# The order of a first mixer's end: sums, a pause of VectorE, two turned banks read late, and a weight block in another tile

## The chip, the cores and the metric

The kernel runs on one core of one Trainium2 chip, as one program. The metric is the device time of one execution in microseconds (us). Five engines work side by side, each through its own queue in order: TensorE (PE; matmuls and transposes, with its weight loads as PEld), VectorE (DVE), ScalarE (ACT), GpSimd (POOL) and SyncE (SP), which here only issues DMA transfers. An instruction starts when those ahead of it on its engine have started and the semaphores that it waits for are set.

## The reference

Two decoder layers on one sequence of 512 tokens and 1024 columns, in float32. Layer 0 mixes by pooling, layer 1 by a gated unit with a spatial matrix; each is followed by an MLP of 4096 hidden columns with squared ReLU.

```
for i in range(DEPTH):                      # DEPTH = 2
    mod = silu(c) @ ada_w[i] + ada_b[i]
    sh1, sc1, g1, sh2, sc2, g2 = jnp.split(mod, 6, axis=-1)
    h = modulate(rmsnorm(x, norm_mix_g[i]), sh1, sc1)
    y = pool_mixer(...) if i % 3 == 0 else sgu_mixer(...)
    x = x + g1[:, None, :] * y
    h = modulate(rmsnorm(x, norm_mlp_g[i]), sh2, sc2)
    x = x + g2[:, None, :] * square(relu(h @ mlp_w1[i])) @ mlp_w2[i]
return rmsnorm(x, final_g)
```

The change lies in layer 0: from the end of the pooling mixer, over the norm that follows it, into the first half of its MLP.

## The kernel before

**Products.** Every float32 product is made of three matmuls: each operand is split in a high part and the rest, and high × high, high × low and low × high are summed. ScalarE writes a weight block's high part (`wh`, L203), VectorE the rest (`wl`, by subtraction, L204). The tokens' operand is `hb`, `as` or `xh`, `xl`, made in the same two steps.

**The mixer.** A string of names, `WORK`, sets the order in which ScalarE, VectorE and TensorE get their instructions up to 60 us; `LOADS` gives the order of the transfers that SyncE issues. A name's letters say what is done, its digits which of four groups of 256 columns (or which column block) it is done for. `mGJ` and `nKJ` are products of 128 rows of the adaptive weights with the condition (VectorE, L420; the `n` are scale and shift of the MLP's column block K). `prG` is the pooling product (TensorE, L497), `adGH` adds it into the residual x for half H of the tokens (VectorE, L506), `smGT` squares the 256 columns G of token tile T and sums them (ScalarE, L333; with the suffix V on VectorE). `s` and `tot` sum over the groups (VectorE, L561 to L565), and `tot` starts the power -1/2 on GpSimd (L283), whose result is `rr`. `tnG` turns 256 columns of x in eight TensorE transposes into two banks `px` (L520), `tdG` reads them on ScalarE (L524). `diag` (L574, L576) spreads `rr` over diagonal matrices, which TensorE multiplies with ones into the bank `rb` (L577), so that the norm's factor stands beside each column. `nfK` makes mods and scale of block K on ScalarE (L540, L542). `hiK` and `loK` split the first MLP weights of block K (L551, L554). Ahead of `rb` and of the sweep TensorE runs some matmuls on constants (`busy`, L348).

**The sweep.** The MLP's row blocks 0 to 6 are computed together over eight steps, one for each column block k: 21 matmuls a step. Beside them VectorE and ScalarE make the operand of the next step: norm_hi (VectorE L581, then ScalarE L582), norm_lo (VectorE L586), norm_out (ScalarE L589), two `n`, the split of the next weights. After it `put` (L724) reads each bank with a ReLU into `g`, two halves a bank, in the order 3, 0, 1, 2, 4, 5, 6; then row block 7 follows (`f`), and squares (L716).

**The rest of the first half** goes in units (c, j, m) of a scheme with seven products in place of eight: block pair c, j, product m in the order 1, 5, 6, 3, 2, 7, 4. `b101q` is the bank of products for c = 1, j = 0. Their weights are sums of blocks: a chain tile `ch10q` or `ch11q` starts as block (0, 0), blocks are added into it by VectorE (L781), and one is added by a transfer of GpSimd's queue (L777), which can be issued only when `ch10q` has been read for the unit before. `raw1111q` is block (1, 1) of c = 1, j = 1 in row-block numbers r = 1, n = 1. Blocks lie in a pool of three tiles (`w4`), and some in the tile of the gate's row, which is free here (tag `gb`; the function `in_gb` says which). The `wh`, `wl` tiles are a pool of five. Within this part VectorE, ScalarE and the transfers' issues are put in order by the scheduler; TensorE's order is the program's.

Of the kernel before, what the change touches and what calls it, by code (L numbers as in the profile page):

```python
# [29 lines left out]
UNDER = 16  # L30

RESET = 48

POPS = (3, 3, 3, 2, 2, 1, 1, 1)

# [23 lines left out]
def c_g(n, k):  # L59
# [5 lines left out]

LOADS = """
    x m20 ag2 m22 m21 m23 gt11 pw2 gt10 m12 m10 m13 m11 m33 ag0 m01 pw1 m02 m00 m03 m32 m30 ag3 pw0 m31
    n11 pw3 raw0 n00 n21 n01 raw1
"""

WORK = """
    cab edge sq0 rowc sq2 sq3 sq1V rms m20 m22 rowp m21 m23 gt11 fin2 bandr gm2 win2 we2 gt10 pd2 win1 m12
    pr2 win3 m10 gc1 m11 bc1 ad21 m13 gm0 ad20 sm23 fin1 m33 we1 pd1 win0 m01 sm22 m02 m00 m03 pr1 ad10
    fin0 pd0 m32 gm3 m30 we0 pr0 m31 fin3 sm10 pd3 ad11 we3 sm21 sm11 hi0 pr3 sm20 ad00 sm13 sm12 sm01
    ad01 sm02 sm03 n00 tn2 sm00 tn0 ad30 s3 ad31 n01 sm30 sm31 sm33 sm32 td2 tot td0 tn3 nf0 n21 n11 tn1  # L80
    diag td3 td1 lo0
"""


GM = [0, 2, 3]
GT = [1]
# [5 lines left out]
def decoder_kernel(ctx: ExitStack, tc: tile.TileContext, xtok, vecs, rows, fgrow, ada0, adag, ada1, pool_w, w1s, w1f, w1b, w2, w_v, w_u, w_o, wsT, lnp, bs, out):  # L92
# [200 lines left out]
    with (  # L293
# [285 lines left out]
        def norm_hi(k):  # L579
            t = xf(k)  # L580
            V.scalar_tensor_tensor(t, t, scl[0][1][:, k : k + 1], rbs[0], ALU.mult, ALU.mult)  # L581
            A.activation(H(k, ALL)[0], t, AF.Identity, bias=mod(0, c_sh(1, k)))  # L582
# [15 lines left out]
            diag=spread_norms, hi=sweep_hi, lo=sweep_lo,  # L598
        )
        loads()  # L600
        for op in WORK.split():
            on_v, op = op.endswith("V"), op.rstrip("V")
            kind, d = op.rstrip("0123456789"), [int(c) for c in op if c.isdigit()]
            work[kind](*d, *([V] if on_v else []))
            loads()


        sweep = [bank("po", xz) for _ in range(SWEEP - 4)] + [bank("po") for _ in range(4)]
        busy("sweep", sweep[0])
        for k in range(KD):  # L610
            norm_hi(k)
            if k + 1 < KD:
                queue += [n for n in (f"n{k + 1}0", f"raw{k + 1}", f"n{k + 1}1") if n not in LOADS]
                loads()
                if f"n{k + 1}0" not in WORK:
                    n_(k + 1, 0)
                norm_lo(k)
                sweep_hi(k + 1)
                if f"n{k + 1}1" not in WORK:
# [12 lines left out]
            for f in range(EARLY):  # L632
                T.matmul(sweep[f], wl[:, fs[f]], xh, start=(k == 0), stop=False)
# [60 lines left out]
    def mlp(i, extra, units, final):  # L694
# [23 lines left out]
        def put(f, po):  # L718

            c, q = divmod(f, 8)  # L720
            j, p = divmod(q, 4)
            with tc.high_priority():
                for r in range(2):
                    A.activation(G_(c, r, j)[:, p], po[:, 256 * r : 256 * r + 256], AF.Relu)  # L724

        def squares(f):
            c, q = divmod(f, 8)
# [24 lines left out]
        spare = []  # L752

        def in_gb(c, j, r, n):
            return ((r, n) == (1, 0) and (i, c, j) != (1, 0, 0)) or (i, r, n, j) == (1, 1, 1, 1) and c < 2

        def blk(c, j, r, n):
            if (c, j, r, n) not in blks:
# [200 lines left out]
                more.setdefault(ss_[max(n - LEAD, 0)], []).append(at)  # L959
        real = [n for n, (k, u) in enumerate(units) if k in prep]  # L960
        ready = {}
        for n, (kind, u) in enumerate(units):
            if kind in calls:
                calls[kind](*u)
                continue
            if kind == "x":
                u()
                continue
            x = real.index(n)
            s = 0  # L970
# [392 lines left out]
```

## Time and profile before

| | |
|---|---|
| median of 3 runs | 843.9 us (842.48 to 845.34) |
| profiled execution | 844.26 us |
| its span | 842.6 us |
| granted TensorE clock, mean | 0.997 |
| busy: TensorE, its weight loads | 822.7 us, 727.4 us |
| busy: VectorE, ScalarE, GpSimd | 680.7, 514.9, 114.9 us |
| HBM read, written | 181.49 MB, 6.30 MB |

A row of a timeline gives start and duration in us, engine, line, operation, output<-inputs, shapes and how many like instructions are taken together; in brackets how long the engine stood idle ahead of it and what it then waited for. A row of the list of waits gives the waiting instruction, what it waited for, the time in total, how often, and the longest. Buffer numbers are left out of the names, so different blocks `ch10q` and tiles `g` read alike.

### The profile page before, as it was taken

What the parts mean: (1) busy time and instruction counts of PE and PEld (TensorE: products, weight loads), DVE (VectorE), ACT (ScalarE), POOL (GpSimd) and SP (SyncE); (2) the same over time, 40 slices, a digit from 0 to 9 for tenths busy, and PEclk for the clock granted to TensorE, in tenths of its full rate; (3) what the DMA queues carried; (4) which work ended last, traced back from release to release, by engine and by line L of the source; (5) the groups of instructions that cost most, each with busy time, mean ns of one, the idle gap of its engine ahead of it and who ended that gap; (6) DMA issues with size and microseconds to landing.
All of it is one profiled execution on the core that took longest, in us unless ns stands there. A gap on an engine that the chain in (4) does not pass through costs nothing.

```text
span 842.6 us, 12722 instructions
## 1 busy us (share of the span) xinstructions
PE 822.7 (98%) x4898; PEld 727.4 (86%) x4898; DVE 680.7 (81%) x864; ACT 514.9 (61%) x739; POOL 114.9 (14%) x135
## 2 busy tenths in 40 slices
PE   8999999999999999999999999999999999999996
PEld 7778899999988888888888887999999988888885
DVE  6889889988779867796898776688887678976886
ACT  5276786776755555676232237868677775665562
POOL 3010001000223300021020002011000132321000
PEclk9999999999999999999999999999999999999998
DMA  9999858998999989464856636568988799998502
GB/s 346 407 363 322 298 140 256 268 289 263 290 250 206 194 220 264 137 225 161 253 179 219 225 119 213 137 159 197 294 249 260 199 212 243 193 215 227 161 24 78
DMA packets 51651, 188.62 MB, mean 224 GB/s; under 512 B 5739, under 2 KB 5891, under 8 KB 50566
## 3 DMA queue, kind: packets, MB, share of 16 engines
q1 hardware_dynamic: 37090, 133.52, 43.9%
q0 software_dynamic: 14352, 54.02, 32.9%
q8 instruction: 38, 0.62, 0.3%
q10 hardware_dynamic: 148, 0.27, 0.1%
q14 instruction: 23, 0.19, 0.1%
HBM read 181.49 MB, written 6.30 MB: 223 GB/s over the span
## 4 chain that ended last, share of the span: by engine, by line
PE 65%; DVE 15%; DMA 10%; issue 4%; ACT 4%; POOL 1%; SPq 0%; POOLq 0%; DVEq 0%; ACTq 0%
PE pm L903 28%; PE po L216 12%; DVE wl L204 4%; DMA ada<-in_ada 3%; DMA wh<-in_ada 2%; PE b311q L216 2%; PE b305q L903 2%; PE b315q L903 2%; DVE ada L240 2%; PE b301q L216 2%; DVE ada L420 2%; PE b101q L216 1%; PE b315q L216 1%; PE b201q L216 1%; PE b305q L216 1%
## 5 line engine op out<-in xcount | busy, mean ns | idle before, releaser
L903 PE MATMUL pm<-wh,o 128*128 128x512 f32 x736 | 182.2, 390 | 0.0
L903 PEld LDWEIGHTS pm<-wh,o 128*128 128x128 f32 x736 | 137.8, 188 | 28.7
L903 PE MATMUL pm<-wl,o 128*128 128x512 f32 x368 | 98.4, 389 | 0.0
L203 ACT ACTIVATE wh<-bt 128x1024 fp32r<-128x1024 f32 x64 | 67.3, 1057 | 45.5 <-PE pm L903 36.1
L204 DVE TENSOR_TENSOR wl<-bt,wh 128x1024 fp32r<-128x1024 f32 x64 | 77.8, 1220 | 16.4 <-ACT wh L203 16.3
L903 PEld LDWEIGHTS pm<-wl,o 128*128 128x128 f32 x368 | 69.1, 188 | 14.3
L240 DVE SCALAR_TENSOR_TENSOR ada<-ada,cb 128x1024 f32<-128x1024 f32 x56 | 68.0, 1219 | 9.5 <-DMA ada<-in_ada 9.2
L662 DVE TENSOR_TENSOR o<-g,o 128x1024 fp32r<-128x1024 f32 x56 | 68.3, 1219 | 6.2 <-ACT o L661 6.2
L216 PE MATMUL po<-hb,wh 128*128 128x512 f32 x224 | 69.1, 389 | 0.0
L661 ACT ACTIVATE o<-g 128x1024 fp32r<-128x1024 f32 x56 | 58.7, 1048 | 10.6 <-PE pm L903 7.4
L203 ACT ACTIVATE wh<-b 128x1024 fp32r<-128x1024 f32 x32 | 34.0, 1062 | 37.6 <-PE pm L903 31.4
L204 DVE TENSOR_TENSOR wl<-b,wh 128x1024 fp32r<-128x1024 f32 x32 | 39.2, 1224 | 21.3 <-ACT wh L203 21.3
L882 POOL DMA_DIRECT2D bt<-in_w x48 | 41.5, 897 | 105.4 <-DVE wl L204 100.5
L203 ACT ACTIVATE wh<-raw 128x1024 fp32r<-128x1024 f32 x33 | 34.9, 1059 | 32.7 <-PE pm L903 13.5
L204 DVE TENSOR_TENSOR wl<-raw,wh 128x1024 fp32r<-128x1024 f32 x33 | 40.2, 1222 | 13.6 <-ACT wh L203 13.5
L216 PEld LDWEIGHTS po<-hb,wh 128*128 128x128 f32 x224 | 42.1, 188 | 8.6
L216 PE MATMUL po<-hb,wl 128*128 128x512 f32 x112 | 44.1, 394 | 0.2 <-ACT g L724 0.2
L716 ACT ACTIVATE g<-g 128x512 f32<-128x512 f32 (+1 forms) x72 | 41.1, 601 | 1.1
L216 PE MATMUL po<-wh,gt 128*128 128x512 f32 x128 | 39.9, 390 | 0.0
L216 PE MATMUL po<-wh,hb 128*128 128x512 f32 x128 | 39.8, 390 | 0.0
L997 ACT ACTIVATE tmp<-x 128x512 f32<-128x512 f32 (+1 forms) x24 | 14.8, 619 | 26.0 <-DVE x L989 21.7
L216 PEld LDWEIGHTS po<-wh,gt 128*128 128x128 f32 x128 | 24.0, 188 | 5.0
(477 smaller groups left out, 2108.7 us busy)
## 6 DMA issues: line engine op xcount, KB each, us to landing
ada<-in_ada SPq DMA_DIRECT2D x72, 512.0 KB, 4.6
bt<-in_w POOLq DMA_DIRECT2D x48, 512.0 KB, 10.5
bt<-in_w SPq DMA_DIRECT2D x16, 512.0 KB, 6.7
raw<-in_w SPq DMA_DIRECT2D x16, 512.0 KB, 6.7
b<-in_w SPq DMA_DIRECT2D x16, 512.0 KB, 10.0
b<-in_w POOLq DMA_DIRECT2D x16, 512.0 KB, 10.2
wh<-in_ada SPq DMA_DIRECT2D x9, 512.0 KB, 9.9
wl<-in_ada SPq DMA_DIRECT2D x9, 512.0 KB, 9.9
```

The source lines that it names most:

```text
L203: A.activation(h[:, c], r[:, c], AF.Copy)
L204: V.tensor_tensor(l[:, c], r[:, c], f32(h[:, c]), ALU.subtract)
L216: T.matmul(o[:, c], a, b[:, c], start=first and q == 0 and not c.start, stop=last and q == 2 and c.stop is None, **kw)
L240: keep(V.scalar_tensor_tensor(r, r, 1.0, cb, ALU.mult, ALU.mult, accum_out=pmv[i, b][:, j : j + 1]))
L420: V.scalar_tensor_tensor(r, r, 1.0, cb, ALU.mult, ALU.mult, accum_out=out)
L661: A.activation(o[0], a, AF.Copy)
L662: V.tensor_tensor(o[1], a, f32(o[0]), ALU.subtract)
L716: A.activation(t, t, AF.Square)
L882: G.dma_start(r, piece(c, *nxt, q), accum_op=ALU.add)
L903: T.matmul(banks[hf], o[a][:, 2 * q + p, hf], w[q][b][:, S * p : S * p + S], start=start and q + n + p == 0, stop=stop and q + n + p == 4, ...
L997: A.activation(tmp, xt, AF.Square, scale=D**-0.5, accum_out=o)
```

## The change

It reorders the two strings, runs the last two reads of turned banks (`WORK0`) inside the sweep's first step, lets three units' weights be prepared ahead of the puts, keeps the first put's place in the program's order, and lets `raw1111q` use the gate row's tile. (The lines of the strings are cut to what the prediction speaks of.)

```diff
+FIRST = 3
...
 LOADS = """
...
-    n11 pw3 raw0 n00 n21 n01 raw1
+    pw3 raw0 n00 n01 n10 n11 raw1
...
-    ad01 sm02 sm03 n00 tn2 sm00 tn0 ad30 s3 ad31 n01 sm30 sm31 sm33 sm32 td2 tot td0 tn3 nf0 n21 n11 tn1
-    diag td3 td1 lo0
+    sm00 sm01 sm02 n00 tn0 sm03 tn2 ad30 lo0 ad31 sm30 sm31 sm33V s3 sm32 td0 tot tn1 diag td2 tn3 n01 nf0
...
+WORK0 = "td1 td3"
...
             norm_hi(k)
+            if k == 0:
+                run(WORK0)
             if k + 1 < KD:
...
                 for r in range(2):
-                    A.activation(G_(c, r, j)[:, p], po[:, 256 * r : 256 * r + 256], AF.Relu)
+                    ins = A.activation(G_(c, r, j)[:, p], po[:, 256 * r : 256 * r + 256], AF.Relu)
+                    if (i, f, r) == (0, FIRST, 0):
+                        tc.keep_in_program_order(ins)
...
         def in_gb(c, j, r, n):
-            return ((r, n) == (1, 0) and (i, c, j) != (1, 0, 0)) or (i, r, n, j) == (1, 1, 1, 1) and c < 2
+            return ((r, n) == (1, 0) and (i, c, j) != (1, 0, 0)) or (r, n, j) == (1, 1, 1) and (i == 1 and c < 2 or (i, c) == (0, 1))
...
+        def ahead(count):
+            for m in real[:count]:
+                ready[m] = prep[units[m][0]](units[m][1])
+
+        calls["pre"] = ahead
...
-    us = [("cl", (1,)), ("cl", (2,))] + [("put", (f, sweep[f])) for f in (3, 0, 1, 2, 4, 5, 6)] + [("f", 7), ("a", (0,))]
+    us = [("cl", (1,)), ("cl", (2,)), ("pre", (3,))] + [("put", (f, sweep[f])) for f in (3, 0, 1, 2, 4, 5, 6)] + [("f", 7), ("a", (0,))]
```

What stands in the engines' queues shows it best. VectorE at the mixer's end, before (`x_100` is half 1 of x, `pm_483` the adaptive columns of block 0, `pm_535` and `pm_537` those of later blocks):

```order
L561 TENSOR_REDUCE s_167<-ssg 128x4
L562 TENSOR_SCALAR s_167<-s_167 128x4
L506 TENSOR_TENSOR x_100<-x_100,po 128x2x256
L420 SCALAR_TENSOR_TENSOR ada,pm_483<-ada,cb 128x1024
L565 TENSOR_TENSOR s_167<-s_167,ssg 128x4
L420 SCALAR_TENSOR_TENSOR ada,pm_535<-ada,cb 128x1024
L420 SCALAR_TENSOR_TENSOR wh,pm_537<-wh,cb 128x1024
L574 TENSOR_SCALAR diag<-ident,rr 128x128 x2
L554 TENSOR_TENSOR wl<-raw,wh 128x896
```

and now:

```order
L505 TENSOR_TENSOR x_99<-x_99,po 128x2x256
L553 TENSOR_TENSOR wl<-raw,wh 128x896
L505 TENSOR_TENSOR x_100<-x_100,po 128x2x256
L334 SCALAR_TENSOR_TENSOR sq_149,ssg<-x_100 128x256
L560 TENSOR_REDUCE s_167<-ssg 128x4
L561 TENSOR_SCALAR s_167<-s_167 128x4
L564 TENSOR_TENSOR s_167<-s_167,ssg 128x4
L573 TENSOR_SCALAR diag<-ident,rr 128x128 x2
L419 SCALAR_TENSOR_TENSOR wl,pm_483<-wl,cb 128x1024
L580 SCALAR_TENSOR_TENSOR h_102<-h_102,scl_92,rb 128x512
```

The split of the first weights (L553) has come ahead of the last addition and the sums behind it, one square is VectorE's own, and between the total (L564) and diag no adaptive column is left.

TensorE at the same place, before, from the third turn on (two rows a turn; `cab` is a constant, so these rows are the dummies):

```order
L520 MATMUL px<-ident,x_99 128x128 x4
L520 MATMUL px<-ident,x_100 128x128 x4
L520 MATMUL px<-ident,x_99 128x128 x4
L520 MATMUL px<-ident,x_100 128x128 x4
L348 MATMUL rb<-cab,ones 128x256 x2
L577 MATMUL rb<-diag,ones 128x128 x4
L348 MATMUL po<-cab,ones 128x256 x4
```

and now:

```order
L519 MATMUL px<-ident,x_99 128x128 x4
L519 MATMUL px<-ident,x_100 128x128 x4
L347 MATMUL rb<-cab,ones 128x256 x2
L576 MATMUL rb<-diag,ones 128x128 x4
L519 MATMUL px<-ident,x_99 128x128 x4
L519 MATMUL px<-ident,x_100 128x128 x4
L347 MATMUL po<-cab,ones 128x256 x4
```

The fourth turn has gone from ahead of `rb` and its dummies to behind them; the third still stands ahead.

ScalarE at the puts, before:

```order
L589 ACTIVATE h_103<-h_103,mods_89 128x512
L203 ACTIVATE wh<-ch10q 128x1024
L203 ACTIVATE wh<-gb 128x1024
L203 ACTIVATE wh<-ch11q 128x1024
L724 ACTIVATE g<-po 128x256 x14
L661 ACTIVATE as<-h_102 128x1024
L716 ACTIVATE g<-g 128x256 x2
L203 ACTIVATE wh<-raw1110q 128x1024
```

and now:

```order
L588 ACTIVATE h_103<-h_103,mods_89 128x512
L729 ACTIVATE g<-po 128x256 x6
L202 ACTIVATE wh<-ch10q 128x1024
L729 ACTIVATE g<-po 128x256 x4
L202 ACTIVATE wh<-gb 128x1024
L729 ACTIVATE g<-po 128x256 x4
L202 ACTIVATE wh<-ch11q 128x1024
L666 ACTIVATE as<-h_102 128x1024
L721 ACTIVATE g<-g 128x256 x5
```

The three `wh` stood ahead of all puts and stand between them now.

VectorE in the units, from the subtraction for `raw1001q` to the one for `g<-g,b101q` that unit (1, 0, 4) waits for, before:

```order
L204 TENSOR_TENSOR wl<-raw1001q,wh 128x1024
L816 TENSOR_TENSOR g<-g,b112q 128x512
L204 TENSOR_TENSOR wl<-ch11q,wh 128x1024
L657 TENSOR_TENSOR g<-g 128x1024
L781 TENSOR_TENSOR ch11q<-ch11q,raw1111q 128x1024
L204 TENSOR_TENSOR wl<-ch10q,wh 128x1024
L240 SCALAR_TENSOR_TENSOR ada,pmv<-ada,cb 128x1024
L204 TENSOR_TENSOR wl<-ch11q,wh 128x1024
L818 TENSOR_TENSOR g<-b105q,g 128x512
L240 SCALAR_TENSOR_TENSOR ada,pmv<-ada,cb 128x1024
L204 TENSOR_TENSOR wl<-raw1111q,wh 128x1024
L820 TENSOR_TENSOR g<-g,b101q 128x512
```

and now:

```order
L203 TENSOR_TENSOR wl<-raw1001q,wh 128x1024
L667 TENSOR_TENSOR as<-h_103,as 128x1024
L203 TENSOR_TENSOR wl<-ch11q,wh 128x1024
L667 TENSOR_TENSOR hb<-h_102,hb 128x2x256
L203 TENSOR_TENSOR wl<-ch10q,wh 128x1024
L239 SCALAR_TENSOR_TENSOR ada,pmv<-ada,cb 128x1024
L667 TENSOR_TENSOR hb<-h_102,hb 128x2x256
L788 TENSOR_TENSOR ch11q<-ch11q,raw1111q 128x1024
L825 TENSOR_TENSOR g<-b105q,g 128x512
L239 SCALAR_TENSOR_TENSOR ada,pmv<-ada,cb 128x1024
L203 TENSOR_TENSOR wl<-ch11q,wh 128x1024
L827 TENSOR_TENSOR g<-g,b101q 128x512
```

The sum of two `g` (L657) and `wl<-raw1111q` have gone further back, behind this piece, an `as` has come in, the addition of `raw1111q` stands behind `wl<-ch10q` instead of ahead, and the two halves of `hb` stand apart, with `wl<-ch10q` and a column between them.

ScalarE around the second reading of `ch10q`, before:

```order
L716 ACTIVATE g<-g 128x512
L814 ACTIVATE g<-b105q 128x512
L203 ACTIVATE wh<-ch10q 128x1024
L814 ACTIVATE g<-b101q 128x512
L203 ACTIVATE wh<-ch11q 128x1024
```

and now:

```order
L721 ACTIVATE g<-g 128x512
L821 ACTIVATE g<-b105q 128x512
L202 ACTIVATE wh<-ch10q 128x1024
L721 ACTIVATE g<-g 128x256 x3
L821 ACTIVATE g<-b101q 128x512
L202 ACTIVATE wh<-ch11q 128x1024
```

Three squares have come between `wh<-ch10q` and the read of `b101q`.

More of the change, by code (lines that the diff above doesn't have):

```diff
@@ L78 @@
     pr2 win3 m10 gc1 m11 bc1 ad21 m13 gm0 ad20 sm23 fin1 m33 we1 pd1 win0 m01 sm22 m02 m00 m03 pr1 ad10
-    fin0 pd0 m32 gm3 m30 we0 pr0 m31 fin3 sm10 pd3 ad11 we3 sm21 sm11 hi0 pr3 sm20 ad00 sm13 sm12 sm01
-    ad01 sm02 sm03 n00 tn2 sm00 tn0 ad30 s3 ad31 n01 sm30 sm31 sm33 sm32 td2 tot td0 tn3 nf0 n21 n11 tn1
-    diag td3 td1 lo0
+    fin0 pd0 sm20 sm21 sm10 sm11 m32 gm3 ad11 m30 we0 pr0 sm12 sm13 m31 fin3 pd3 we3 hi0 ad00 pr3 ad01
+    sm00 sm01 sm02 n00 tn0 sm03 tn2 ad30 lo0 ad31 sm30 sm31 sm33V s3 sm32 td0 tot tn1 diag td2 tn3 n01 nf0
 """
+WORK0 = "td1 td3"
 GM = [0, 2, 3]
@@ L600, in decoder_kernel, with run @@
         loads()
[L601 to L605, printed above, removed]
+        def run(ops):
+            for op in ops.split():
+                on_v, op = op.endswith("V"), op.rstrip("V")
+                kind, d = op.rstrip("0123456789"), [int(c) for c in op if c.isdigit()]
+                work[kind](*d, *([V] if on_v else []))
+                loads()
+        run(WORK)
         sweep = [bank("po", xz) for _ in range(SWEEP - 4)] + [bank("po") for _ in range(4)]
@@ L614, in decoder_kernel @@
                 loads()
-                if f"n{k + 1}0" not in WORK:
+                if f"n{k + 1}0" not in WORK + WORK0:
                     n_(k + 1, 0)
@@ L618, in decoder_kernel @@
                 sweep_hi(k + 1)
-                if f"n{k + 1}1" not in WORK:
+                if f"n{k + 1}1" not in WORK + WORK0:
                     n_(k + 1, 1)
```

## The prediction

> **What bounds the kernel now.** I read the page first: which engine fills the span.
>
> ```profile
> span 842.6 us, 12722 instructions
> PE 822.7 (98%) x4898; PEld 727.4 (86%) x4898; DVE 680.7 (81%) x864; ACT 514.9 (61%) x739; POOL 114.9 (14%) x135
> ```
>
> TensorE has work for 98% of the span, and the diff takes no matmul away and adds none. So the change can only move TensorE's idle time, about 20 us in all. The list of waits on TensorE says which of it lies where the diff reaches:
>
> ```profile
> PE b101q L216 <- DVE g L820: 1.1, 1, 1.1
> PE b101q L216 <- ACT g L814: 0.8, 1, 0.8
> ```
>
> Both are single waits in the first MLP (at 125 and 132 us). A third, of 1.40 us, lies at the end of the first mixer and is seen in the first rows of part 1. Then came the timelines around them, quoted with each part. The sum is made against the profiled execution, 844.26 us (span 842.6 us), which is 0.36 us above the median 843.9 of the three timed runs; the forecast is set against the median. About 0.3%, or 2.5 us, is what a measurement can tell from no change.
>
> **Part 1: the mixer's end.** TensorE, ScalarE, VectorE and GpSimd in the timeline, from the last product to the sweep's first matmul:
>
> ```profile
> 51.47 1.91 PE L520 MATMUL px<-ident,x 128*128 128x128 f32 x16
> 54.78 2.33 PE L520 MATMUL px<-ident,x 128*128 128x128 f32 x16 [1.40 <-ACT h L524]
> 56.95 1.03 PE L348 MATMUL rb<-cab,ones 128*128 128x256 f32 x4
> 57.82 1.05 PE L577 MATMUL rb<-diag,ones 128*128 128x128 f32 x8
> 58.71 1.89 PE L348 MATMUL po<-cab,ones 128*128 128x256 f32 x8
> 60.55 0.50 PE L633 MATMUL po<-hb,wl 128*128 128x512 f32 x1
> 65.59 0.39 PE L633 MATMUL po<-hb,wl 128*128 128x512 f32 x1
> ```
>
> ```profile
> 53.73 0.42 ACT L333 ACTIVATE sq<-x 128x256 f32<-128x256 f32 x1
> 54.15 2.04 ACT L524 ACTIVATE h<-px 128x512 f32<-128x512 f32 x4
> 56.70 0.69 ACT L576 ACTIVATE diag<-ident,rr 128x128 f32<-128x128 f32 x2
> 60.40 0.94 ACT L551 ACTIVATE wh<-raw 128x896 fp32r<-128x896 f32 x1
> ```
>
> ```profile
> 52.11 0.17 DVE L561 TENSOR_REDUCE s<-ssg 128x4 f32<-128x12 f32 x1 [1.46 <-ACT sq L333]
> 52.38 0.68 DVE L506 TENSOR_TENSOR x<-x,po 128x512 f32<-128x512 f32 x1
> 54.27 0.17 DVE L565 TENSOR_TENSOR s<-s,ssg 128x4 f32<-128x4 f32 x1
> 58.99 0.75 DVE L581 SCALAR_TENSOR_TENSOR h<-h,scl,rb 128x512 f32<-128x512 f32 x1 [0.87 <-PE rb L577]
> 61.46 1.08 DVE L554 TENSOR_TENSOR wl<-raw,wh 128x896 fp32r<-128x896 f32 x1
> ```
>
> ```profile
> 54.53 1.95 POOL L283 TENSOR_TENSOR rr<-s,mhalf 128x4 f32<-128x4 f32 x1 [2.81 <-DVE s L565]
> ```
>
> The last addition into x (ad31, 52.38) stood behind the sum (52.11), and that stood 1.46 us waiting for squares. The new order puts lo0 there (1.08 us, as at 61.46), behind the addition that the 1.46 us follow, so ad31 starts at about 51.75, and ends at 52.4. Only one square of it (0.42 us at 53.73, with the next instruction right behind) is left on ScalarE, the other goes to VectorE beside it; with three sums of at most 0.17 us the total is there at about 53.2 instead of 54.27: **1.1 us sooner**.
>
> The power on GpSimd follows at 53.4. It took 1.95 us beside VectorE's wide operations; now VectorE stands still for it. The nearest rows for that are the last four powers of the kernel, in a stage with fewer such operations:
>
> ```profile
> L283 POOL TENSOR_TENSOR rr<-sums,mhalf x4: 545/887/1527, 817.0 to 836.4; 128x1 f32<-128x1 f32 x4
> ```
>
> Their tile's row gives 545, 887 and 1527 ns (shortest, median, longest). I take 0.9 us, with 0.55 and 1.95 as ends: rr at 54.3 (54.0 to 55.35). [...]
>
> What TensorE does then: a turn is 8 transposes, 0.95 us (1.91 for 16). Two run at 51.47 as before. The third needs banks that ScalarE reads behind its last square: two reads of 0.5 us from 53.0, so it ends at about 55.1. The dummies ahead of rb take 0.87 us (56.95 to 57.82): 56.0. The rb matmuls, for which diag (0.69 us behind rr) is ready at 55.0 to 56.05, take 0.89: 56.9. The fourth turn is now behind them, 0.95: 57.85. The sweep's dummies take 1.84 (58.71 to 60.55): the sweep starts at 59.7 to 59.8 instead of 60.55. The operands are there before: norm_hi at 57.0 behind rb, or behind the scale, which ScalarE now makes after diag (0.69), two reads (1.0) and the mods (mods and scale fill the 0.6 us from the reads' end at 56.1 to 56.70): 2.4 us behind rr, 56.7 to 57.8. Then 0.75 us and some 0.7 for hb: 58.5 to 59.3. So the early power is not worth all of its 1 us: TensorE's own dummies take over. **−0.8 us** (−0.5 to −0.8).
>
> **Part 2: two turned banks read late.** Four reads, 2.04 us by the row of 54.15, now stand on ScalarE between the first hb and wh of step 1. Queued behind them: wh (0.94), wl on VectorE (1.08), norm_hi (0.75), hb (0.7). From hb at 58.5 that chain ends at 64.0. TensorE comes to step 1 at about 64.8 (65.59 less 0.8). **0**; if the power stays at 1.95 us the chain ends at 64.8, just then, and a further delay counts in full: up to +0.4. The adaptive columns that moved out of the pause lie in steps 0 and 1 beside TensorE's 5 us a step (60.55 to 65.59), two in a step as in later steps of the old order.
>
> **Part 3: the puts.** ScalarE and TensorE at the sweep's end:
>
> ```profile
> 97.48 3.93 ACT L724 ACTIVATE g<-po 128x256 f32<-128x256 f32 x14
> 98.46 0.61 PE L216 MATMUL po<-hb,wh 128*128 128x512 f32 x2
> 99.26 0.50 PE L216 MATMUL po<-hb,wl 128*128 128x512 f32 x1 [0.18 <-ACT g L724]
> ```
>
> Two matmuls of 0.39 last 0.61, so one follows the other after 0.22, and row block 7 was due at 98.9: it lost 0.35 us to a put. Its bank now waits for the eighth put instead of the sixth, but one wh (about 1 us) stands ahead, not three. The last step's 21 matmuls start at 94.2, with the shift at 93.4, and the first two banks are complete six matmuls later, at 94.8. Eight puts of 0.28 (3.93 for 14) and one wh end then at 98.1, just as TensorE comes. I take **−0.15** (−0.35 to +0.2), −0.95 in all here.
>
> **Part 4: the sum-up transfer and the two b101q waits.** GpSimd's queue issues ch10q, a transfer that adds into its tile; the rows from it to TensorE:
>
> ```profile
> 115.19 0.86 POOL L777 DMA_DIRECT2D ch10q<-in_w1b  x1 [12.27 <-DVE wl L204]
> ```
>
> ```profile
> 116.12 1.34 ACT L716 ACTIVATE g<-g 128x256 f32<-128x256 f32 x4
> 123.36 1.06 ACT L203 ACTIVATE wh<-ch10q 128x1024 fp32r<-128x1024 f32 x1 [2.90 <-DMA ch10q<-in_w1b]
> 124.33 0.58 ACT L814 ACTIVATE g<-b101q 128x512 f32<-128x512 f32 x1
> ```
>
> ```profile
> 95.71 1.23 DVE L204 TENSOR_TENSOR wl<-ch10q,wh 128x1024 fp32r<-128x1024 f32 x1 [1.81 <-ACT wh L203]
> 123.60 1.23 DVE L781 TENSOR_TENSOR ch11q<-ch11q,raw1111q 128x1024 f32<-128x1024 f32 x1 [2.69 <-DMA raw1111q<-in_w1b]
> 131.04 0.68 DVE L820 TENSOR_TENSOR g<-g,b101q 128x512 f32<-128x512 f32 x1
> ```
>
> ```profile
> 124.96 0.39 PE L216 MATMUL b101q<-hb,wl 128*128 128x256 f32 x1 [0.81 <-ACT g L814]
> 131.77 0.38 PE L216 MATMUL b101q<-hb,wl 128*128 128x256 f32 x1 [1.09 <-DVE g L820]
> ```
>
> The transfer was issued at 115.19 and landed at 123.36, 8.15 us later. The extremes of its tile and the median of GpSimd's queue in the page are:
>
> ```profile
> DMA to landing us min/median/max: 5.5/6.8/8.2
> bt<-in_w POOLq DMA_DIRECT2D x48, 512.0 KB, 10.5
> ```
>
> Its issue waits for a wl on VectorE. Two instructions of 1.2 us that stood before this wl stand after it now (−2.4); the first wl of the row, that of 95.71, starts 1.8 us later, since its wh is behind six puts from 94.8 (+1.8). I take 0.65 us sooner (0 to 1.2). Its neighbours in the queues stay: where raw1111q was loaded beside it, raw2001q is now. So 8.15 us again: landed at 122.7. Then wh 0.97 (123.36 to 124.33), three squares which stand now ahead of the read of b101q (0.335 each), and 0.63 from the read's start to TensorE (124.33 to 124.96): 125.3. TensorE's old loss was 0.97, 0.81 of it in the matmul's row and the rest in its weight load; it is due at 124.96 less 0.97 less 0.95, or 123.05: **2.2 us lost where 0.97 was**. Second, hb's later half, which was long done, now stands on VectorE behind that wl and an adaptive column (1.2 each), and takes 0.6: ready at 126.65. TensorE wants it, by my estimate, 0.8 us into the block, at 126.1: **0.5 to 0.8**. Against it, the next wait goes: at 131.77 TensorE lost 1.25 (1.09 of it in the matmul's row) to g<-g,b101q. Its VectorE row is now made up of wl, column, half hb, an addition, g, column, wl and g behind 123.65: three of 0.6 and five of 1.2, done at 131.45, with TensorE there at 131.55. Sum at this point: −0.95 + 2.2 − 0.97 + 0.7 − 1.25 = **−0.3**. Every microsecond of landing goes through in full.
>
> **Part 5: what VectorE has still to do.** The addition of raw1111q (behind 123.60 in the old idle time), a sum of two g, 1.2 us each, and half hb (0.6) are 3.0 us more behind 123.65, where the row that wl leads began at 124.8: +1.85. Where it can be caught up, and where it next counts:
>
> ```profile
> 134.52 1.23 DVE L204 TENSOR_TENSOR wl<-ch20q,wh 128x1024 fp32r<-128x1024 f32 x1 [0.45 <-ACT wh L203]
> 149.98 1.23 DVE L204 TENSOR_TENSOR wl<-raw2001q,wh 128x1024 fp32r<-128x1024 f32 x1 [0.45 <-ACT wh L203]
> 163.62 0.68 DVE L820 TENSOR_TENSOR g<-g,b201q 128x512 f32<-128x512 f32 x1
> ```
>
> ```profile
> 164.52 0.28 PE L216 MATMUL b201q<-hb,wl 128*128 128x256 f32 x1
> ```
>
> The two idle times take 0.9, so g<-g,b201q (163.62, 0.68 long) comes 0.95 us late; TensorE had 0.2 us to spare. It then starts at 165.2 instead of 164.52: **+0.7** in all, between −0.3 (all caught up) and +1.6 (nothing). From there the instructions of all engines stand as before, so the shift stays.
>
> The sum: 844.26 + 0.7 = 845.0 against the profiled execution, or 844.6 against the median. I say **844.5**.
>
> **The rivals.** *Faster*: the transfer lands after 5.5 us, the short end of its tile. Then no block of b101q waits, and m4 is 0.95 + 0.97 + 1.25 = 3.1 us ahead. If VectorE's rows behind it also keep up, the kernel takes 840.8; if they don't, g<-g,b201q is some 2 us late and only 1 us is left (842.9). For it: the tile's own range. Against: the issue meets the same neighbours. [...] Chance 0.13.
>
> *Slower*: the transfer meets more traffic, since the loads of later blocks have moved towards it, and takes the 10.5 us of GpSimd's other loads. wh<-ch10q stands at the head of ScalarE's row, with squares and the read of b101q behind it, so all 2.35 us go to TensorE: +3.05, 846.95. It decides (over 0.3%) from 10.0 us on. Chance 0.14.
>
> *The change doesn't do what it says*: the earlier total is eaten, because the fourth turn, the dummies and the four late reads hold the sweep where it was. Then 0.8 us are missing in each row that follows: 845.3. For it: TensorE's own chain was within 0.1 us of setting the start. Chance 0.15. The forecast keeps 0.58.
>
> **How the numbers follow.** The forecast's own terms (−0.3 to +0.4, ±0.5 and −1.0 to +0.9) give 843 to 846. The rivals' ends are 840.8 and 846.95; leaving out two in ten, the range is 841.8 to 847.0. Faster by over 0.3% (below 841.4) needs the fast transfer and a VectorE that keeps up: 0.08, and 0.06 for terms that I sized too high. Slower (above 846.4): 0.12 of the slow transfer, 0.04 of unabsorbed VectorE work. The rest, 0.70, is the same.
>
> **What the new profile would show.** Right: the power at 0.6 to 0.9 us near 53.4, the sweep's first matmul at 59.8, no idle time in front of step 1, the landing of ch10q near 122.7 and a wait of about 2 us for the read of b101q, the wait for g<-g,b101q gone, one of about 1 us for g<-g,b201q. Wrong: a first matmul at 60.3 or later (parts 1 and 2), a landing before 121 or after 124 (part 4), TensorE without a wait at b201q (part 5).

## The result and the profile after

| | before | after |
|---|---|---|
| median of 18 runs | 844.85 us (842.48 to 848.68) | 848.19 us (844.53 to 852.29) |
| profiled execution, span | 844.26, 842.6 us | 847.72, 846.0 us |

The ratio after to before is **1.0042, 95% interval 1.0030 to 1.0053**: slower by some 3.5 us, where 844.5 us and no measurable change were forecast. 848.19 us lies above the range given (to 847.0). The page of after begins:

```profile
span 846.0 us, 12726 instructions
PE 826.6 (98%) x4898; PEld 731.0 (86%) x4898; DVE 681.2 (81%) x866; ACT 513.9 (61%) x737; POOL 114.2 (13%) x135
```

The number of matmuls is the same, yet TensorE is busy 3.9 us longer (822.7 before): it is not only its waits that grew, its matmuls took more time. The list of waits on TensorE of after, cut to the rows of the first MLP's half:

```profile
PE b201q L215 <- DVE g L827: 3.3, 1, 3.3
PE b105q L215 <- ACT g L821: 1.7, 1, 1.7
PE b101q L215 <- ACT g L821: 1.4, 1, 1.4
...
PE b101q L215 <- DVE hb L667: 0.5, 1, 0.5
```

Two waits of 1.1 and 0.8 us have become four of 6.9 us. TensorE's timeline, from the third turn to the sweep and then at those four waits:

```profile
54.62 1.03 PE L347 MATMUL rb<-cab,ones 128*128 128x256 f32 x4
...
56.37 1.04 PE L519 MATMUL px<-ident,x 128*128 128x128 f32 x8
57.24 1.89 PE L347 MATMUL po<-cab,ones 128*128 128x256 f32 x8
58.79 0.58 PE L638 MATMUL po<-hb,wl 128*128 128x512 f32 x1
...
121.06 0.39 PE L215 MATMUL b105q<-as,wl 128*128 128x256 f32 x1 [1.71 <-ACT g L821]
125.53 0.39 PE L215 MATMUL b101q<-hb,wl 128*128 128x256 f32 x1 [1.37 <-ACT g L821]
127.14 0.50 PE L215 MATMUL b101q<-hb,wh 128*128 128x256 f32 x2 [0.53 <-DVE hb L667]
168.21 0.58 PE L215 MATMUL b201q<-hb,wl 128*128 128x256 f32 x1 [3.28 <-DVE g L827]
```

Set against the starts in before, TensorE is 1.76 us ahead at the sweep (60.55), 2.08 us ahead at the first b101q block (104.83), 0.2 us ahead at 121.06, 0.57 us behind at 125.53 (124.96) and 0.1 behind at unit (1, 0, 4) (131.77). So the mixer's gain was made, and was gone at 125 us. At 162.04 TensorE is 0.24 us behind (161.80), at the next block, 168.21 (164.52), 3.69 us, and the block behind that one starts 6.26 us late (173.50 for 167.24). The windows of after around it (last three columns: granted clock, share of the DMA engines, GB/s) say why:

```profile
166.00:168.00 2.00, 0.00 (x0) 0.00 (x0) 1.67 (x2) 1.25 (x2) 0.15 (x1) 0.74 0.82 324
168.00:170.00 2.00, 1.79 (x8) 1.79 (x9) 2.00 (x4) 1.78 (x4) 0.71 (x1) 0.50 0.53 53
170.00:172.00 2.00, 2.00 (x11) 2.00 (x10) 2.00 (x4) 0.94 (x1) 0.00 (x0) 0.50 0.90 180
172.00:174.00 2.00, 2.00 (x12) 2.00 (x12) 0.95 (x3) 0.26 (x1) 0.00 (x0) 0.55 0.97 348
174.00:176.00 2.00, 2.00 (x20) 2.00 (x19) 0.68 (x1) 1.80 (x3) 0.00 (x0) 1.00 1.03 397
```

The clock falls to 0.50 at about 167, still within the wait, and stays there for some 6.8 us, with 11 matmuls in 2 us instead of 20: the block at 168.21 takes 5.29 us, and 2.72 in before. TensorE is then 6.4 us late and stays so to 200 us. At the end it is 3.46 us late: 1.4 us come back up to 223 us, where before waits once more (0.4 us at b301q) and its blocks take 2.83 us to after's 2.72, and the rest in layer 1; no edit lies there, and the experiments don't follow it.

Why VectorE came so late to b201q stands in its row and in SyncE's. VectorE of after:

```profile
124.11 1.23 DVE L203 TENSOR_TENSOR wl<-ch10q,wh 128x1024 fp32r<-128x1024 f32 x1 [1.86 <-ACT wh L202]
...
140.79 1.23 DVE L239 SCALAR_TENSOR_TENSOR ada<-ada,cb 128x1024 f32<-128x1024 f32 x1 [1.06 <-DMA ada<-in_ada]
...
151.92 1.22 DVE L203 TENSOR_TENSOR wl<-raw2001q,wh 128x1024 fp32r<-128x1024 f32 x1
155.17 1.22 DVE L239 SCALAR_TENSOR_TENSOR ada<-ada,cb 128x1024 f32<-128x1024 f32 x1 [2.03 <-DMA ada<-in_ada]
...
167.48 0.68 DVE L827 TENSOR_TENSOR g<-g,b201q 128x512 f32<-128x512 f32 x1
```

Two waits for adaptive columns' loads, of 1.06 and 2.03 us, stand here that before's profile doesn't have. SyncE's queue, before and then after:

```profile
98.10 0.33 SPq L762 DMA_DIRECT2D raw1110q<-in_w1b  x1
106.02 0.33 SPq L762 DMA_DIRECT2D raw2010q<-in_w1b  x1
127.13 3.21 SPq L1090 DMA_DIRECT2D ada<-in_ada  x2
```

```profile
100.25 0.33 SPq L769 DMA_DIRECT2D raw1110q<-in_w1b  x1
126.51 0.33 SPq L1103 DMA_DIRECT2D ada<-in_ada  x1
132.93 0.33 SPq L769 DMA_DIRECT2D raw2010q<-in_w1b  x1
133.31 2.23 SPq L1103 DMA_DIRECT2D ada<-in_ada  x2
...
142.05 6.83 SPq L1103 DMA_DIRECT2D ada<-in_ada  x2
```

raw1111q has taken raw2010q's place in the gate row's tile, so raw2010q now waits until raw1111q has been split (VectorE, 131.68 to 132.9), and a column's load is queued behind it: it goes out at 133.31, where the second load of the row of 127.13 went out at 130.0. That is the load that VectorE waits for at 140.79. The load waited for at 155.17 is a later one, the second of the row of 142.05, issued at 148.55.

### The profile page after: what moved, and what is told of

Its sections match the earlier page's. It is cut to its first block, busy times and chain, and to the rows that moved or that the text cites. A ratio compares the mean times of both kernels' runs of the same rounds, so it can differ in the third digit from the quotient of the medians.

```text
span 846.0 us, 12726 instructions
## 1 busy us (share of the span) xinstructions
PE 826.6 (98%) x4898; PEld 731.0 (86%) x4898; DVE 681.2 (81%) x866; ACT 513.9 (61%) x737; POOL 114.2 (13%) x135
## 4 chain that ended last, share of the span: by engine, by line
PE 81%; DVE 9%; DMA 4%; issue 3%; ACT 2%; POOL 0%; POOLq 0%; DVEq 0%; SPq 0%; ACTq 0%
PE pm L910 28%; PE po L215 16%; PE b301q L215 3%; PE b311q L215 3%; DVE wl L203 3%; PE b315q L910 2%; PE b305q L910 2%; PE b211q L215 2%; DMA ada<-in_ada 2%; PE b215q L215 2%; PE b201q L215 2%; PE b305q L215 2%; PE b205q L215 1%; PE b101q L215 1%; PE b111q L215 1%
## 5 line engine op out<-in xcount | busy, mean ns | idle before, releaser
L215 PEld LDWEIGHTS po<-wh,hb 128*128 128x128 f32 x128 | 24.0, 188 | 5.0
## 6 DMA issues: line engine op xcount, KB each, us to landing
bt<-in_w POOLq DMA_DIRECT2D x48, 512.0 KB, 10.5
```

What stands on the lines that cost most here:

```text
L215: T.matmul(o[:, c], a, b[:, c], start=first and q == 0 and not c.start, stop=last and q == 2 and c.stop is None, **kw)
```

## The experiments

Each ratio is to the kernel before on the same chip; 0.001 is 0.84 us.

**The tile's part of the change.** First the changed kernel with the issue of raw2010q moved behind the next adaptive column's load, all other rows as they were:

```diff
-            if spare and (u == ss_[0] or in_gb(...)):
+            late_gb = i == 0 and u == (1, 1, 3)
+            if spare and not late_gb and (u == ss_[0] or u == (1, 1, 7) and i == 0 or in_gb(...)):
```

> The changed kernel with one issue moved: SyncE issues the load of raw2010q behind the adaptive column's load that it now stands ahead of; every other row of every engine is as in the changed kernel. Queue theory: the gate tile's new block makes raw2010q wait for wl<-raw1111q (131.7 to 132.9) at the head of SyncE's row, the column's load behind it goes out 3 us late, VectorE waits 1.06 us for it at 140.8 and 2.03 us for the next but one at 155.2, and TensorE 3.28 us at b201q. Then the first wait goes (under 0.2 us), the second falls under 1.2, b201q's wait falls to 0.3 to 1.5, and the time is 1.8 to 3 us below the changed kernel's (ratio to before 1.0005 to 1.002). Backlog theory (part 5 of the prediction): VectorE's three more instructions behind wl<-ch10q make the wait; they stay, so b201q still waits over 2.5 us and the ratio stays near 1.004.

Measured: 1.0026 (1.0010 to 1.0041). The first column's wait is gone, the second is not. VectorE there, and TensorE at the block ahead of b201q and at b201q:

```profile
155.05 1.23 DVE L239 SCALAR_TENSOR_TENSOR ada<-ada,cb 128x1024 f32<-128x1024 f32 x1 [2.19 <-DMA ada<-in_ada]
```

```profile
163.44 0.28 PE L215 MATMUL b211q<-hb,wl 128*128 128x256 f32 x1
...
168.09 0.39 PE L215 MATMUL b201q<-hb,wl 128*128 128x256 f32 x1 [1.77 <-DVE g L828]
```

The wait at b201q is 1.77 us for 3.28, but the block starts only 0.12 us sooner (168.09 for 168.21). The wait is shorter because TensorE comes 1.4 us later (163.44 for 162.04): in this profile the clock fell at 126 already.

```profile
124.00:126.00 2.00, 1.01 (x7) 0.88 (x7) 2.00 (x4) 0.94 (x3) 0.00 (x0) 1.00 0.14 23
126.00:128.00 2.00, 1.47 (x7) 1.40 (x7) 2.00 (x3) 0.29 (x1) 0.00 (x0) 0.61 1.05 293
```

So the queue behind raw2010q makes the first column's wait, and hardly anything of the loss at b201q. Second, the changed kernel with the old rule for the tile:

```diff
-            return ... or (r, n, j) == (1, 1, 1) and (i == 1 and c < 2 or (i, c) == (0, 1))
+            return ... or (i, r, n, j) == (1, 1, 1, 1) and c < 2
```

> The changed kernel with the old rule for the gate row's tile: raw1111q goes to the pool of three again, raw2010q is loaded early. The rows of VectorE and ScalarE are those of the changed kernel. Queue theory: as in the run with raw2010q behind the column, b201q waits 0.3 to 1.5 us, ratio to before 1.0005 to 1.002; raw1111q lands at 123.5 to 124.5, before its addition at 127. Backlog theory: b201q waits over 2.5 us, ratio near 1.004.

Measured: 1.0028 (1.0015 to 1.0041). No column waits near 140, but the second wait is there again, and b201q waits 2.48 us and starts at 167.81:

```profile
154.77 1.23 DVE L239 SCALAR_TENSOR_TENSOR ada<-ada,cb 128x1024 f32<-128x1024 f32 x1 [2.03 <-DMA ada<-in_ada]
```

So the tile's share of the 3.69 us is 0.4 us, or 1.0 if one counts from wl<-ch10q, which starts 0.62 us later here. Both ratios are some 1.3 us below that of the whole change, with intervals that overlap its own, and outside what either theory gave. And the new rule alone in the kernel before (the same line, the other way):

> The kernel before with the new rule for the gate row's tile alone. Queue theory: VectorE waits for a column near 140 and again near 153, b201q waits 1 to 3 us, ratio to before 1.001 to 1.003. Backlog theory: VectorE has not more to do, and its wait of 2.69 us for raw1111q at 123.6 goes: ratio 0.999 to 1.000 and no wait at b201q.

Measured: **0.9980 (0.9966 to 0.9993)**, 1.7 us faster than before. The tile by itself does no harm to the time, though its profile shows what the queue theory said: a column's load stands right behind raw2010q (131.48 behind 131.10), VectorE waits 1.46 and 1.19 us for columns at 139.55 and 153.49, and b201q starts 2.0 us later than in before (166.53), after a wait of 0.8 us. This is the one version here whose interval lies below that of before; where its 1.7 us come from is not shown, since its profiled execution (844.89 us) is no shorter than that of before, and beside the new mixer (below) the tile brings nothing.

**The mixer's end.** The three strings alone in the kernel before, with no `pre`, no `FIRST` and the old tile rule:

```diff
-FIRST = 3
+FIRST = None
-    us = [("cl", (1,)), ("cl", (2,)), ("pre", (3,))] + ...
+    us = [("cl", (1,)), ("cl", (2,))] + ...
```

> The kernel before with the new strings of the mixer's end alone (squares, pause, two turned banks late, loads): no units prepared ahead of the puts, the old rule for the gate row's tile. The sweep starts at 58.8 instead of 60.55 in either theory. The scheduler reorders puts and units by itself here: eight puts, one wh, six puts. Queue theory: no load of raw2010q ahead of a column, so no column wait over 0.5 us, ratio 0.998 to 0.9995. Backlog theory: the half hb, the addition of raw1111q and the sum of two g stand behind wl<-ch10q here too, so b201q waits over 2 us and the ratio is 1.001 to 1.003.

Measured: 1.0027 (1.0012 to 1.0043). The sweep starts 2.2 us sooner (58.37), but the scheduler, which sees other times, orders the rows behind the sweep anew: eight puts, one wh, six puts. b101q then waits 3.35 and 1.01 us, and the clock is 0.50 from 127.0 to 133.8 us. No column waits, and b201q doesn't either: neither theory had the place of the loss. To part the two, the next kernel has the new mixer, but VectorE, ScalarE and SyncE keep the order of before behind the sweep:

```diff
+    for seq in PINNED:      # the order of before, engine by engine
+        for a, b in zip(seq, seq[1:]):
+            tc.add_manual_dep(by[f"I-{base + b}"], f"I-{base + a}", ...NoSync...)
```

> The new mixer's end alone, with VectorE's, ScalarE's and SyncE's rows behind it written out as they stand in the kernel before, so the scheduler changes nothing behind the sweep. Order theory: the loss of the changed kernel lies in the rows that the scheduler set anew behind the sweep, and the mixer's end itself brings its 1.5 to 1.9 us at the sweep's start, of which the waits at 125 and 132 us leave 0.8 to 1.8: ratio 0.998 to 0.999. Pacing theory: the landing of ch10q and ScalarE's row set the times at 125 and 132 us whatever comes sooner, so that the two waits on b101q grow by what the sweep gained: ratio 0.9995 to 1.001.

Measured: 1.0005 (0.9984 to 1.0025). The gain ends at row block 7, whose bank waits for a put behind three wh:

```profile
100.04 0.50 PE L224 MATMUL po<-hb,wl 128*128 128x512 f32 x1 [2.67 <-ACT g L738]
```

And the other half: the old mixer, with the rows behind the sweep held in the order of after, tile included.

> The old mixer's end, and behind it the rows of VectorE, ScalarE and SyncE written out as they stand in the changed kernel, raw1111q in the gate row's tile included. Order theory: the loss without the gain, a wait of 2.5 us or more at b201q and a stretch at half the granted clock behind it: ratio 1.003 to 1.006. Pacing theory: these rows do no harm by themselves, they were late only against a sweep that starts sooner: ratio 0.999 to 1.001.

Measured: **1.0042 (1.0027 to 1.0058)**, the ratio of the whole change, without its mixer. Its longest wait:

```profile
PE b201q L230 <- DVE g L842: 2.4, 1, 2.4
```

b201q starts at 167.86 here. So the loss lies in the rows behind the sweep as a whole, and the mixer's 1.76 us are worth nothing to them. The new mixer with the new tile, the rows held as with the tile alone:

> The new mixer's end and the new rule for the gate row's tile, with the rows behind the sweep as in the run of that rule alone (0.998 of before). Order theory: both gains add, ratio 0.996 to 0.9975. Pacing theory: only the tile's gain, 0.998 to 0.999.

Measured: 1.0002 (0.9986 to 1.0018), row block 7 waits 2.29 us. That is neither forecast: beside the 1.0005 of the new mixer without the tile, the tile's gain doesn't come again. Is the place of the puts all that is missing? Two versions of that kernel put the puts ahead of the wh (eight, wh, six, wh, wh; and six, wh, four, wh, four, wh), by editing only ScalarE's list:

```diff
-    [29, 33, 40, 48, 11, 13, 15, 8, 12, 10, 18, 14, 21, 16, 20, 23, 22, 24, ...
+    [29, 11, 13, 15, 8, 12, 10, 18, 14, 33, 21, 16, 20, 23, 22, 24, 40, 48, ...
```

> New mixer end and new tile for gb, rows behind the sweep as in the kernel before, but eight of the fourteen puts stand ahead of the wh from ch10q and six ahead of the wh from gb, instead of all behind three wh. Theory (the mixer's gain is lost only at the puts): the wait of f7, 2.29 us, is gone, TensorE enters the first b101q block 1.5 to 2 us ahead of the kernel before, and what is left of it at the end is 1 to 2 us: ratio 0.997 to 0.998. Rival (the pace is set by ScalarE's and VectorE's rows and the landings behind them): the time lost at f7 comes back as waits at b101q and b201q, ratio 1.000 as with the puts late; it would be 1.002 if a wait over 3 us draws the clock down.

> As the kernel with eight puts first, but with six puts, wh, four, wh, four, wh, wh, the mixture that the changed kernel has. Theory (gain lost only at the puts): f7 waits up to 0.3 us, ratio 0.997 to 0.998. Rival (rows behind set the pace): the wh stand later than with the old order, b101q and b201q wait in place of f7, ratio 1.000.

Measured: 1.0024 (1.0005 to 1.0043) and 0.9999 (0.9984 to 1.0013). TensorE was 2.3 to 2.4 us ahead at the first b101q block, and was behind the kernel before at the second b105q block (by 2.2 and 1.5 us). The largest wait of the first of the two, and of the second alike:

```profile
PE b105q L224 <- ACT g L830: 2.8, 1, 2.8
```

The rival's mechanism holds: behind the sweep ScalarE and VectorE set the pace, and what TensorE has gained it waits for some blocks later. Its ratio holds for the second; why the first is slower is not shown, since its profiled execution was a short one (844.34 us) in which the clock didn't fall.

**The clock.** The changed kernel with 22 matmuls ahead of the block that waits at b201q. They write into a bank that a later block clears:

```diff
+            if (i, u) == (0, (2, 0, 4)):
+                ZS[2, 1] = bank("b215q", ps)
+                for _ in range(22):
+                    T.matmul(ZS[2, 1][:, 0:256], wv[0][:, 0, 0:P], asums.of[m](0)[0], start=True, stop=True)
```

> The changed kernel with 22 matmuls more, which write a bank that is not in use, put into TensorE's row at the place where it waits 3.28 us at b201q (2.5 us of work in place of idle time). Clock theory: the wait halves the granted clock for some 6 us behind it, which costs about 2.7 us; with work in the wait the clock stays at 1.00 there and the time falls by 1 to 2.7 us, ratio to before 1.001 to 1.003, though more is computed. Rival: VectorE is what is late, and the slow stretch only lets it catch up: the waits behind grow by what the clock brings, ratio 1.004 as in the changed kernel.

Measured: 1.0026 (1.0010 to 1.0043), 1.3 us below the changed kernel, with intervals that overlap. In its profile neither the wait nor the low clock is left at b201q, but another stretch of 0.50 follows the waits of 1.40 and 0.52 us at 126 to 127. So the next kernel fills the waits at b105q and b101q too (14 and 11 matmuls):

> The changed kernel with idle-filling matmuls at all three places: 14 ahead of the second b105q block (its wait was 1.71 us), 11 ahead of the b101q block behind it (1.37 us), 22 ahead of b201q (3.28 us). They write into banks that a later block clears, so nothing is left out. All other rows stay. Theory (the clock is the rest of the loss): no 1 us stretch between 115 and 180 us shows 0.50, the profile has no wait over 1 us there, and the ratio comes to about 1.001, 1.5 us under the kernel that fills b201q alone. Rival (the waits cost their own length and nothing else): the granted clock is no part of it, and the ratio stays at 1.0026, that of the kernel that fills b201q alone, since the waits are only filled, not shortened.

Measured: 1.0038 (1.0024 to 1.0052). The clock side's 1.001 lies outside; the rival's 1.0026 lies inside, but not for its reason. The three waits are gone, and in their place:

```profile
PE b101q L217 <- DVE g L835: 2.1, 1, 2.1
```

```profile
134.00:136.00 2.00, 2.00 (x12) 2.00 (x11) 1.77 (x3) 1.97 (x4) 0.00 (x0) 0.50 1.02 303
```

VectorE sets the next time, and a wait of 2.1 us was enough for the clock to fall. Filling waits in after can't tell the wait and the clock apart, because they move. So the wait was made in the kernel before, with all rows up to b201q as they were, by extra readings of b201q on VectorE that change nothing:

```diff
                     V.tensor_tensor(t, t, po, ALU.subtract)
+                    if (i, u) == (0, (2, 0, 7)):
+                        for _ in range(2):
+                            V.scalar_tensor_tensor(t, po, 0.0, t, ALU.mult, ALU.add)
```

> The kernel before, with nothing changed but that b201q is held longer: two extra VectorE instructions read it (they add zero times the bank to g) and stand behind a wl and an adaptive column, so its bank comes free about 3.3 us later, at 167.8 instead of 164.3. TensorE then waits about 3.3 us there, as it does in the changed kernel, with all rows around it as before. Theory (the clock falls behind such a wait, and takes more time than the wait): a stretch of 5 to 7 us at 0.50 follows it in the profile, the shift behind it is 3.3 + 2.5 us or more, and the ratio is 1.005 or above. Rival (a wait costs its own length): no such stretch, the shift is 3.3 us, less 1 us that later waits give back: ratio 1.003 or below.

The same with 24 filling matmuls, and with one reading in place of two:

> The same with 24 matmuls (2.7 us) ahead of that block, which write into a bank that a later block clears. The block starts at the same time, 167.8. Theory (clock): no stretch at 0.50, ratio 2 to 3 us below the kernel without the filling, 1.003 or below. Rival (a wait costs its own length): the same ratio as without the filling, to 0.05%.

> The same with one extra instruction behind one wl: b201q comes free about 1.75 us later and TensorE waits about 1.5 us. Theory (the clock falls only behind a long wait): no stretch at 0.50, the shift is 1.5 us, ratio 1.001 to 1.002. Rival (each wait over 1 us draws the clock down): a stretch at 0.50 and a ratio of 1.003 or above.

Measured, in that order: **1.0051 (1.0032 to 1.0070), 1.0032 (1.0015 to 1.0050), 1.0015 (1.0000 to 1.0030)**. The waits of the three, and the windows behind them of the first two:

```profile
PE b201q L218 <- DVE g L825: 3.4, 1, 3.4
```

```profile
168.00:170.00 2.00, 1.04 (x5) 1.05 (x6) 2.00 (x6) 1.03 (x2) 0.00 (x0) 0.55 1.03 215
170.00:172.00 2.00, 2.00 (x11) 2.00 (x11) 1.41 (x5) 0.23 (x1) 0.00 (x0) 0.50 0.87 277
...
174.00:176.00 2.00, 2.00 (x15) 2.00 (x14) 0.00 (x0) 1.52 (x3) 0.00 (x0) 0.71 0.92 367
```

```profile
PE b201q L219 <- DVE g L830: 2.1, 1, 2.1
```

```profile
170.00:172.00 2.00, 2.00 (x15) 2.00 (x14) 1.77 (x5) 0.60 (x1) 0.00 (x0) 0.69 0.92 305
172.00:174.00 2.00, 2.00 (x11) 2.00 (x11) 0.00 (x0) 0.35 (x1) 0.00 (x0) 0.50 0.87 287
```

```profile
PE b201q L218 <- DVE g L825: 1.5, 1, 1.5
```

(The first of these profiles is of an execution with a clock of 0.95 from start to end, the longest of the twelve; its total is not used, only its fall to 0.50.) A wait of 1.5 us has no stretch of 0.50 behind it and costs 1.3 us (0.0015 of 845), about its own length. The two readings cost 4.3 us. What of that goes beyond the length of the wait is not shown: in the profile TensorE came to b201q at 165.4, held up by the lower clock, and would come there about 1 us sooner at 1.00 (164.4 in the filled kernel) and so wait longer than 3.4 us. Filled to a wait of 2.1 us, the block starts no sooner (169.32, for 168.96), and still the clock falls, which neither side had said; but the stretch is half as long, 3.4 us for 6.8, and the cost is 2.7 us. So the shorter stretch would be worth 1.6 us (by the medians, 849.96 and 847.92, 2.0), with intervals that overlap. The fall of the clock is seen; its price at the spot can be read from the blocks behind it, which took 2.7 us more in after (5.29 and 2.88 us, 2.72 each at the full clock) and 1.75 us more in the filled kernel (4.09 and 3.10). What of it reaches the end is an estimate of 1 to 3 us.

## Why the prediction was wrong

**Part 1, the mixer's end: right in kind, too small.** The sweep came 1.76 us sooner, for 0.8 forecast. The power took about what was said:

```profile
53.39 1.04 POOL L282 TENSOR_TENSOR rr<-s,mhalf 128x4 f32<-128x4 f32 x1 [1.76 <-DVE s L564]
```

1.04 us where 0.9 was taken, beside a VectorE that waits for it (1.17 us, ahead of diag); in before it took 1.95 us, beside VectorE's wide operations. That is one power each. The range's end of 0.5 us was an estimate for a power of 1.95 us beside a VectorE that stands still, which no run here shows. The mis-sized term is TensorE's own: the third turn ended at 54.6 (55.1 forecast), and the fourth turn and the dummies took 56.37 to 58.79, which is 2.4 us and not 2.8. The rival that the sweep stays where it was is refuted.

**Part 2: right.** TensorE has no wait in front of step 1.

**Part 3: right in size, wrong in worth.** No put holds row block 7 in after: the lead grows by 0.32 us, within the range given, and TensorE is 2.08 us ahead at the first b101q block (0.95 forecast). But the pinned kernels show that such a lead ends at row block 7 or at b105q, whichever the puts allow.

**Part 4: one wait was missing.** The transfer did much as said (issue, then landing and what follows on ScalarE):

```profile
115.92 0.86 POOL L784 DMA_DIRECT2D ch10q<-in_w1b  x1 [10.30 <-DVE wl L203]
```

```profile
106.58 1.06 ACT L202 ACTIVATE wh<-raw1110q 128x1024 fp32r<-128x1024 f32 x1 [2.62 <-DMA raw1110q<-in_w1b]
...
120.42 0.59 ACT L821 ACTIVATE g<-b105q 128x512 f32<-128x512 f32 x1
123.02 1.06 ACT L202 ACTIVATE wh<-ch10q 128x1024 fp32r<-128x1024 f32 x1 [2.01 <-DMA ch10q<-in_w1b]
```

It landed at 123.0 (122.7 forecast), but by two errors that nearly cancel: it took 7.1 us and not 8.15, and its issue came 0.7 us later than before instead of 0.65 sooner. The half of hb cost 0.53 (0.5 to 0.8 forecast), and the wait for g<-g,b101q is gone, as said. What the step left out is the row of 106.58. SyncE's load of raw1110q goes into the gate row's tile, and so waits for the subtraction that reads the tile last, whose wh stands among the puts now:

```profile
99.00 1.22 DVE L203 TENSOR_TENSOR wl<-gb,wh 128x1024 fp32r<-128x1024 f32 x1
...
107.68 1.23 DVE L203 TENSOR_TENSOR wl<-raw1110q,wh 128x1024 fp32r<-128x1024 f32 x1 [2.36 <-ACT wh L202]
```

The load was issued at its end, 100.25, 2.15 us later than before, and took 6.3 us. VectorE then stood idle for it for 2.36 us, ahead of the wl on which the transfer's issue waits. ScalarE stood idle for 2.62 us and then had no gap until the read of b105q at 120.42, so TensorE waited 1.71 us there; together with 1.37 and 0.53 that is 3.6 us (4.4 by the starts, with the weight loads) where 2.9 were forecast. As the lead was 2.08 us and not 0.95, the errors nearly cancel: −0.3 was forecast at unit (1, 0, 4), and +0.1 measured. The transfer's 7.1 us lie between the two rivals' 5.5 and 10.5, so neither took place; that the slow rival's 846.95 us come nearest to the 848.19 measured is chance.

**Part 5: the step that failed.** It set VectorE's added work, 3.0 us, against 0.9 us of idle time, and put TensorE 0.7 us late at b201q, with +1.6 as the worst. Measured is 3.69. The work and the idle time came out nearly as said: the two idle times of 0.45 us are gone in after, and at wl<-raw2001q VectorE is 1.94 us late (151.92 for 149.98), 0.9 without the column's wait of 1.06 ahead of it, where 0.95 was forecast. What the step put at nothing, without a reason, is VectorE's waits for the loads of adaptive columns: 1.06 us and then 2.03, with which g<-g,b201q is 3.86 us late (167.48 for 163.62).

The first wait comes of the tile, by raw2010q in SyncE's queue; it is gone in the two kernels that take raw2010q out of the way. The second is not explained by the tile, for these two have it at 2.19 and 2.03 us, and it is not the change's alone: the two kernels with two readings, whose VectorE has the order of before up to b201q, have it at 0.98 and 1.73 us. The longer of these:

```profile
152.80 1.22 DVE L243 SCALAR_TENSOR_TENSOR ada<-ada,cb 128x1024 f32<-128x1024 f32 x1 [1.73 <-DMA ada<-in_ada]
```

The load is issued when VectorE has read an earlier column (148.55 in after, 146.07 in before), so a late VectorE also makes its own load late; why it then took 6.6 us in after, too long to hide, stays open.

**The clock had no term.** The forecast priced a wait at its length. Around waits of 2.1 to 3.4 us the granted clock fell to 0.50, in after's profile for 6.8 us, and TensorE's shift grew from 3.69 to 6.42 us. The stretch lasted 6.8 us in the kernel with two readings too, and 3.4 us in the filled kernel. The length of the wait alone didn't settle whether one came: a single wait of 2.1 us had a stretch with it in two kernels, while waits of up to 2.79 us in others had none.

Of the 3.5 us in all, the rows behind the sweep account for the whole, by the kernel with the old mixer and those rows. How they divide into waits and clock is not settled closer than the estimate above, since the stretch is not in every profile: that of this same kernel, of one of its short executions (846.45 us), shows none, and the mean clock of after's eighteen executions lies between 0.991 and 0.997. The executions agree with a price of that size. Of after's eighteen, the two with a mean clock of 0.997, that of before's profile, took 844.53 and 845.44 us, and the twelve at 0.994 or less a median of 848.6; of the nine with the old mixer, the four at 0.997 or more took 846.4 to 847.8 us and the five below it 848.1 to 850.3. That is no proof: in the kernel with three fillings the five at 0.997 alone spread from 845.4 to 848.5.

## What to carry to other kernels

Where an order is made by a scheduler from times, an earlier start can set everything behind it anew (here a sweep 2.2 us sooner did); cost the new rows on every queue, the one that issues loads too, and ask which engine sets the pace there before counting the gain. A load that waits for a tile holds the loads behind it (a column's, behind raw2010q, went out at 133.31 for 130.0), so a new tenant of a shared tile is priced by what is queued behind the next one. A shorter wait is not yet a gain, since an engine that comes later waits less (with raw2010q moved, 1.77 us for 3.28 at b201q, and a start only 0.12 us sooner): compare the times at which the waiting block starts. A single wait of TensorE of 1.5 us cost 1.3 us here, about its length; with two of the eight of 2.1 to 2.8 us the clock fell to 0.50 as well, and with all three of 3.28 to 3.4 us.

## What the runs showed of the hardware

The granted clock fell to 0.50 around some waits of TensorE and not around others of like length. In the first half of this MLP all three waits over 3 us had a fall with them (3.28 us in after, 3.35 with the new strings alone, 3.4 with two readings). Of eight single waits of 2.1 to 2.8 us two had (2.1 us each: the three fillings, and two readings with filling), and six had not: 2.29, 2.4, 2.48, 2.67 and twice 2.79 us, the last in the two kernels with the puts ahead. Of five pairs of 1.3 to 1.5 and 0.5 us within 3 us two had: the one of 1.30 and 0.53 us in the kernel with raw2010q moved (its windows stand there) and the one of 1.40 and 0.52 us in the kernel with 22 matmuls. The stretches lasted 6.8 us with the three waits over 3 us, and 3.4 us with the other four. A single profile with or without one is therefore one draw, and only the medians of many runs price it.
